# Keeping bf16 copies of the weights in DRAM: what it did to an eight-core encoder layer

## The chip, the cores and the metric

The kernel runs on all 8 cores of one Trainium2 chip. The metric is device time in microseconds (us) of the slowest core, lower is better. Each core works on two of the 16 sequences. No core talks to another, and each loads all weights for itself.

Some executions fall into a slower state: 6 of the 20 runs of the kernel before took 3124 to 3275 us, the others 2898 to 2923, and in a slow run of transfers_alone (3327 us) the four cores of one die had a mean granted clock of 0.81, the others 0.98. 12 of the 14 kernels had such runs. Ratios compare fast runs alone, of both kernels and from the same chip. The plain medians are over all runs of a kernel, slow ones too.

## The reference, cut to what matters

```python
# per layer, x: (16, 2048, 1024) float32, D_FF = 2816
x <- x + 1/2 * SwiGLU_1(RMSNorm(x))
h = RMSNorm(x); proj = h @ w_in            # one projection for all head groups
fox = forgetting attention (8 heads x 64, causal)
gla = gated linear attention (4 heads), rms-normed, times silu(g_out)
x <- x + concat(fox, gla) @ w_out
x <- x + 1/2 * SwiGLU_2(RMSNorm(x))
return RMSNorm(x)
```

The weights arrive as float32. The matmuls use bf16.

## The kernel before

A core treats its 4096 tokens as 8 groups of 512. The stages are FFN1, mixer (projections, attention, output projection) and FFN2, written f1, mixer and f2 below. The kernel does not hold the weight tiles on the chip; every group loads every weight again: 22 `wgu` tiles and 16 `wd` tiles for each FFN, 16 `mixw` tiles for the mixer. The loads go through POOL's DMA queue, which casts float32 to bf16 on the way (it wrote 344 MB, and 705 MB were read from HBM in all).

```python
wgu = sb("wgu", [128, 3, 2048], BF16)             # ring of 3
wd = sb("wd", [128, 4, NC2 * 128], BF16)          # ring of 4
mixw = sb("mixw_t", [128, 2, 2048], BF16)         # ring of 2
...
t1f = rstdM                                       # scratch of the gate tanh: the FFN norm's tile
...
wb = nxt("wgu", 3)
DMA("pool", ("wgu", wb), wgu[:, wb, :], wgu_d[f][half * NC2 + cl], 1 << 20, writes=[("wgu", wb)], ...)
...                                               # 16 matmuls of 128x512 with this tile, tanh, two products

def ffn2(tg, middle):
    ...
    norm_rstd(rstdM[:], "rstdM", b, 0)            # writes rstdM
    ...                                           # x_sb scaled by rstdM, then stored to y by SP

def mixer(tgg):
    ...
    def ev(b, h=h):                               # the output gate, 4 times a group
        tg_ = t1f
        ACTV([(tg_[:], banks[b][:], AF.Tanh, None, 0.5)], [], [PS(b), "rstdM"])
        STT(cc[:, 4 + h, :], tg_[:], 1.0, banks[b][:], ALU.add, ALU.mult, ["rstdM"], [PS(b), ("cc", 4 + h)])
```

The program does not write instructions in the order of execution. It records every operation with what it reads and writes. A planner then simulates the engines with rough durations, and each engine's fixed order comes from that plan.

## Time and profile before

| | before |
|---|---|
| median of the first 6 runs (one of them slow) | 2903.84 us (2898.38 to 3275.29) |
| TensorE (PE) busy in the profiled run | 2693.8 of 2911.3 us |
| PE idle (difference) | 217.5 us |
| of it, waiting for weight DMA (wgu, mixw, wd) | 93.9 us |

In the views, PE is TensorE's matmuls and PEld its weight loads, DVE is VectorE, ACT is ScalarE, POOL is GpSimd. SP is SyncE, which here only issues transfers. L299 is line 299 of the kernel; where a helper makes every instruction, all have its line, so go by the tiles. A `bank` is one of the eight PSUM buffers that matmuls write. "A <- B" among the waits means that A stood idle until B was done.

From the page of the kernel before: busy time by engine (us, share of the span, instructions), then the two main DMA queues (packets, MB, share of 16 engines' time), then HBM traffic.

```profile
PE 2693.8 (93%) x13328; PEld 1260.1 (43%) x13328; DVE 1464.2 (50%) x2186; ACT 1105.4 (38%) x2189; POOL 511.8 (18%) x1017
...
q0 software_dynamic: 106176, 344.07, 72.2%
q1 hardware_dynamic: 10816, 32.53, 3.5%
...
HBM read 704.84 MB, written 16.78 MB: 248 GB/s over the span
```

PE is the bottleneck, 93% busy: 64 uninterrupted matmuls of 128x512 take 14.00 us in the chain of waits, 218.8 ns each, and the granted clock is 0.98 over the span. The DMA engines come second, and 72% of their time goes to the casting queue.

From the list of waits of the kernel before, PE only: total us, times, longest.

```profile
PE bank L299 <- DMA wgu<-wgu: 60.7, 35, 12.2
PE bank L299 <- DMA mixw_t<-mixw: 31.4, 22, 4.3
PE bank L299 <- DVE x_sb L339: 21.7, 18, 2.2
...
PE bank L299 <- DMA wd<-wd: 1.8, 1, 1.8
```

From the page of the kernel before, the DMA issues: count, size, median us from issue to landing.

```profile
wgu<-wgu POOLq DMA_DIRECT2D x352, 512.0 KB, 6.3
wd<-wd POOLq DMA_DIRECT2D x256, 352.0 KB, 5.6
mixw_t<-mixw POOLq DMA_DIRECT2D x128, 512.0 KB, 6.5
```

Compare 6.3 us with the ring. A `wgu` tile feeds 16 matmuls, 3.5 us. In a ring of three, a load issued when its buffer comes free has the time of two other tiles, 7.0 us, before PE needs it. This is an estimate from the durations above, for stretches with FFN work alone.

**Four stretches.** To see where kernels differ, I cut each run by work done, not by time: the moving columns of all PE matmuls are summed, and a stretch ends when 4%, 31%, 86% and 100% of them have been streamed. The times of a stretch are medians over the 8 cores of the profiled run. The second stretch, 4% to 31%, holds nearly all of the stores that the change will add (in the trace after, about 89 of 92 on a core); the fourth is the tail, the last mixer and the last two FFN2.

The windows view of the kernel before, cut at these points on its slowest core. Columns: window, length, busy us (instructions) of PE, PEld, DVE, ACT, POOL, granted PE clock (1.00 is full), mean busy share of the 16 DMA engines, GB/s.

```profile
0.00:148.00 148.00, 113.16 (x485) 47.80 (x486) 56.56 (x79) 31.20 (x48) 27.45 (x66) 0.98 0.90 164
148.00:924.00 776.00, 723.24 (x3718) 346.17 (x3717) 421.53 (x640) 292.78 (x564) 140.98 (x280) 0.99 0.78 129
924.00:2478.00 1554.00, 1472.29 (x7299) 691.78 (x7298) 797.41 (x1192) 614.32 (x1220) 278.73 (x546) 0.98 0.77 133
2478.00:2900.00 422.00, 384.82 (x1831) 174.33 (x1828) 183.30 (x268) 164.53 (x356) 64.61 (x125) 0.96 0.65 113
```

### The profile page before, as it was taken

How to read it: one execution, taken by the hardware profiler on the slowest of the kernel's cores; microseconds unless marked ns; L12 is line 12 of the kernel's file. 1: busy time of each engine (PE TensorE's matmuls, PEld its weight loads, DVE VectorE, ACT ScalarE, POOL GpSimd, SP SyncE). 2: the span in 40 equal slices, each digit the busy share in tenths (PEclk: the TensorE clock that was granted, in tenths of full speed). 3: DMA queues.
4: the chain of work that ended last, by engine and by line, in shares of the span. 5: the costliest groups of instructions: out<-in, count | busy, mean ns of one | idle time of the engine just before them, and what ended most of it. 6: DMA issues, size and time to landing. Idle time of an engine off the chain costs nothing.

```text
span 2911.3 us, 39715 instructions; the slowest of 8 cores (2888.4 to 2911.3 us)
## 1 busy us (share of the span) xinstructions
PE 2693.8 (93%) x13328; PEld 1260.1 (43%) x13328; DVE 1464.2 (50%) x2186; ACT 1105.4 (38%) x2189; POOL 511.8 (18%) x1017
## 2 busy tenths in 40 slices
PE   5999889989999999999999889998999999999797
PEld 2445445434454444444444334543345444354233
DVE  3344845733456444554346735376253664454433
ACT  2231534521437423475234303264231662328611
POOL 1111311211112111121112211122111221111110
PEclk9999999999999999999999999999999999999999
DMA  8988767698785987767877787767887658885365
GB/s 186 143 136 140 114 106 129 109 170 141 128 140 93 177 140 129 122 123 135 137 129 130 138 160 130 133 113 147 135 134 136 111 100 137 154 139 95 75 116 111
DMA packets 117474, 380.17 MB, mean 131 GB/s; under 512 B 13327, under 2 KB 13472, under 8 KB 116384
## 3 DMA queue, kind: packets, MB, share of 16 engines
q0 software_dynamic: 106176, 344.07, 72.2%
q1 hardware_dynamic: 10816, 32.53, 3.5%
q8 instruction: 114, 1.87, 0.3%
q10 hardware_dynamic: 288, 1.05, 0.1%
q14 instruction: 80, 0.66, 0.1%
HBM read 704.84 MB, written 16.78 MB: 248 GB/s over the span
## 4 chain that ended last, share of the span: by engine, by line
PE 71%; DMA 13%; DVE 9%; issue 5%; ACT 2%; DVEq 0%; POOL 0%; SPq 0%; POOLq 0%; ACTq 0%
PE bank L299 71%; DMA wgu<-wgu 6%; DMA mixw_t<-mixw 5%; DVE hM L719 2%; DVE hF L339 2%; DVE x_sb L339 1%; DMA x_sb<-x 1%; DVE hM L339 1%; ACT hM L324 1%; DMA y<-x_sb 1%; DVE Sst L339 1%; DVE thF L339 1%; DVE Sbf L336 1%; ACT L324 1%; ACT rstdM L324 0%
## 5 line engine op out<-in xcount | busy, mean ns | idle before, releaser
L299 PE MATMUL bank<-hF,wgu 128*128 128x512 bf16 x5632 | 1306.2, 385 | 94.6 <-DMA wgu<-wgu 60.7
L299 PEld LDWEIGHTS bank<-hF,wgu 128*128 128x128 bf16 x5632 | 547.4, 99 | 775.2 <-issue 173.4
L299 PE MATMUL bank<-act,wd 128*128 128x512 bf16 x2816 | 644.0, 380 | 23.2 <-DVE x_sb L339 21.2
L324 ACT ACTIVATE thF<-bank 128x512 f32<-128x512 f32 x352 | 209.3, 597 | 830.3 <-PE bank L299 829.4
L339 DVE SCALAR_TENSOR_TENSOR thF<-thF,bank 128x512 f32<-128x512 f32 x352 | 240.7, 686 | 497.9 <-ACT thF L324 495.8
L324 ACT ACTIVATE hM<-bank,biasT 128x256 bf16<-128x256 f32 (+1 forms) x1152 | 435.7, 473 | 125.3 <-PE bank L299 124.4
L299 PEld LDWEIGHTS bank<-act,wd 128*128 128x128 bf16 x2816 | 271.5, 98 | 351.8 <-issue 37.3
L357 POOL DMA_DIRECT2D wgu<-wgu x352 | 189.8, 539 | 1134.1 <-PE bank L299 1110.8
L336 DVE TENSOR_TENSOR act<-bank,thF 128x512 bf16<-128x512 f32 x352 | 242.7, 689 | 233.6 <-PE bank L299 228.6
L339 DVE SCALAR_TENSOR_TENSOR x_sb<-bank,x_sb 128x512 f32<-128x512 f32 x256 | 173.8, 689 | 322.3 <-PE bank L299 321.2
L719 DVE RECIPROCAL hM<-bank 64x128 f32<-64x128 f32 x256 | 244.5, 955 | 65.5 <-PE bank L299 49.2
L324 ACT ACTIVATE sqF<-x_sb 128x512 bf16<-128x512 f32 x192 | 117.0, 627 | 370.9 <-DVE x_sb L339 202.4
L357 POOL DMA_DIRECT2D wd<-wd x256 | 136.8, 535 | 564.7 <-PE bank L299 563.4
L299 PE MATMUL bank<-hM,mixw_t 128*128 128x512 bf16 x896 | 205.3, 383 | 9.4 <-DMA mixw_t<-mixw 8.9
L299 PE MATMUL bank<-hM,V 128*128 128x512 bf16 (+3 forms) x640 | 199.1, 349 | 12.7 <-DVE cc L336 4.6
L299 PE MATMUL bank<-QT,KT 128*128 128x512 bf16 (+3 forms) x640 | 203.2, 350 | 1.5 <-ACT hM L324 1.5
L324 ACT ACT_TABLE_LOAD x93 | 119.3, 1283 | 125.8 <-PE bank L299 116.1
L299 PE MATMUL bank<-mixw_t,hM 128*128 128x256 bf16 x1280 | 149.0, 278 | 12.8 <-DMA mixw_t<-mixw 12.6
L357 POOL DMA_DIRECT2D mixw_t<-mixw x128 | 67.6, 528 | 478.2 <-PE bank L299 444.7
L336 POOL TENSOR_TENSOR hM<-hM,mask 128x128 bf16<-128x128 bf16 x256 | 112.0, 450 | 196.8 <-ACT hM L324 195.6
L299 PEld LDWEIGHTS bank<-mixw_t,hM 128*128 128x128 bf16 x1280 | 126.7, 100 | 37.7 <-issue 18.1
L299 PEld LDWEIGHTS bank<-hM,mixw_t 128*128 128x128 bf16 x896 | 86.8, 99 | 121.3 <-issue 22.8
(90 smaller groups left out, 1373.9 us busy)
## 6 DMA issues: line engine op xcount, KB each, us to landing
wgu<-wgu POOLq DMA_DIRECT2D x352, 512.0 KB, 6.3
wd<-wd POOLq DMA_DIRECT2D x256, 352.0 KB, 5.6
mixw_t<-mixw POOLq DMA_DIRECT2D x128, 512.0 KB, 6.5
y<-x_sb SPq DMA_DIRECT2D x64, 256.0 KB, 10.5
x_sb<-x SPq DMA_DIRECT2D x7, 2048.0 KB, 13.8
x_sb<-x ACTq DMA_DIRECT2D x2, 512.0 KB, 9.7
x_sb<-x SPq DMA_DIRECT2D x2, 512.0 KB, 9.5
wmisct<-wmisc POOLq DMA_DIRECT2D x1, 80.0 KB, 12.2
```

Source lines behind the costliest of these rows:

```text
L299: ins = e.matmul(out, lhsT=l, rhs=r, start=s0, stop=s1)
L324: ins = e.activation(out=out, in_=in_, func=func, **kw)
L336: return DVE(lambda e: e.tensor_tensor(out=out, in0=a, in1=b, op=op), free_n(out), reads, writes, rate, eng, level)
L339: return DVE(lambda e: e.scalar_tensor_tensor(out=out, in0=a, scalar=s, in1=b, op0=op0, op1=op1), free_n(out), reads, writes, level=level)
L357: return P.op(eng, lambda e: e.dma_start(out=out, in_=in_), reads, writes, dma_key=key, dur=1000.0 if eng == "pool" else 70.0, lat=100.0, ...
L719: P.op("dve", lambda e, o_=rcp[drow, qs], i_=banks[ob][srow, qs]: e.reciprocal(out=o_, in_=i_), [], [PS(ob), ("hM", 6), ("hM", 7)], dur=86 ...
```

## The change

The intent: each weight tile is cast once, stored to DRAM in bf16 at its first, second or third use, and loaded in bf16 by SP's hardware queue from then on, with half the bytes to read. 544 of 736 loads move; 92 stores are added. The change also brings four other things: a start gate (the first loads of `wd` and `mixw` and the second group's x wait for a later event than before); later x loads and y stores issued from POOL; new DMA figures in the planner; and another scratch tile for the gate tanh.

```diff
-                dma_free[e] = max(dma_free[e], t + o.dur) + o.nbytes / (o.rate * 1000.0)
-                o.end = dma_free[e] + 2000.0
+                dma_free = max(dma_free, t + o.dur) + o.nbytes / (o.rate * 1000.0)
+                o.end = dma_free + 2000.0 + o.slack
...
+    wgu_s = [dt("wgus%d" % f, [2 * NC2, 128, 2048], BF16, "Internal") for f in range(2)]
+    wd_s = [...]; mixw_s = dt("mixws", ...)
...
-        t1f = rstdM
+        t1f = sqM[:].rearrange("p r t -> p (r t)").bitcast(F32)
...
-                        dur=1000.0 if eng == "pool" else 70.0, ...
+                        dur=700.0 if eng == "pool" else 350.0, ...
...
+        def LOADW(tag, wb, tile, src, keep, i, first, reads=()):
+            key = (tag, keep.tensor.name, i)
+            use = uses.get(key, 0)
+            uses[key] = use + 1
+            kept_at = first + i % 2
+            n = 128 * free_n(tile)
+            if use > kept_at:
+                DMA("sp", (tag, wb, "b"), tile, keep[i], 2 * n, reads=[key], writes=[(tag, wb)])
+                return
+            DMA("pool", (tag, wb), tile, src[i], 4 * n, reads=reads, writes=[(tag, wb)])
+            if use == kept_at:
+                DMA("sp", (tag, wb, "s"), keep[i], tile, 2 * n, reads=[(tag, wb)], writes=[key], level=1)
...
-                    DMA("pool", ("wgu", wb), wgu[:, wb, :], wgu_d[f][half * NC2 + cl], 1 << 20, ...)
+                    LOADW("wgu", wb, wgu[:, wb, :], wgu_d[f], wgu_s[f], half * NC2 + cl, 1 - f, ...)
...  # wd and mixw likewise; their first loads gated on ("act", 5) and ("act", 10)
-            DMA("sp", ("x", xb), ..., rate=0.15)
+            DMA("sp" if tg < 3 else "pool", ("x", xb, tg < 3), ..., slack=8000.0,
+                reads=[("act", 8)] if tg == 1 else ())
...
-                DMA("sp", ("y", k % 4), ...)
+                DMA("sp" if tg < 2 or tg == NTG - 1 else "pool", ...)
...
-                        ACTV([(tg_[:], banks[b][:], AF.Tanh, None, 0.5)], [], [PS(b), "rstdM"])
+                        ACTV([(t1f, banks[b][:], AF.Tanh, None, 0.5)], [], [PS(b), ("sqM", 0), ("sqM", 1)])
```

## The prediction

> **What bounds the kernel now.** TensorE. The page gives PE 93% busy (2693.8 of 2911.3 us), with a granted clock near full speed. Uninterrupted runs in the chain (64 matmuls of 128x512 in 14.0 us) show 219 ns each; all matmuls of the by-shape list, 6.18 million streamed columns, at that rate make about 2640 us, which no DMA change can touch. What is left is 217 us in which PE is idle. The list of PE's waits splits it: weights by DMA 94 us (wgu 60.7, mixw 31.4, wd 1.8), VectorE about 74 us, ScalarE about 33 us. The chain of waits puts 11% of the span on wgu and mixw transfers, but their full flight (6.3 to 6.5 us each) mostly overlaps matmuls; the 94 us is the cost.
>
> Those 94 us by time (waits in windows): 17 us wgu in the first 60 us, about 5 to 170 us, about 8 from 170 to 560, 14.5 at 560 to 710 (the first FFN2, DMA share 0.90), and about 50 us spread over the rest.
>
> **What changes.** 544 of 736 weight loads (264 wgu, 192 wd, 88 mixw) become bf16 loads on SP; 192 remain casting loads on POOL; 92 stores (44 wgu, 32 wd, 16 mixw: 43 MB) are added, in about the first third of the span. From the queue table I work out 0.317 us per software-queue packet (3241 B written, twice that read) and 0.151 us per hardware-queue packet (3008 B): both about 20 GB/s of bytes read per engine. So the gain is the halved read, not the other queue. [...] Estimates: HBM read 705 to about 450 MB, written 17 to about 60 MB, mean DMA share 76% to about 55%; a wgu load lands in about 4 us on SP against 6.3 us. POOL loses 544 issues of 0.53 us, about 290 us of busy time, none of it critical.
>
> [...]
>
> Also: wd, mixw and second-group x loads at the start wait for later events, leaving early bandwidth to wgu; the gate's tanh scratch no longer shares the FFN norm's tile; the scheduler's DMA model changes, which reorders every engine.
>
> **On the critical path.** After about 700 us I expect DMA waits of 50 us to fall to about 8. Each removed wait also saves a pipeline refill (379 ns for an isolated matmul against 219 streaming, 0.16 us), some 6 us. The start saves about 10 us of the 22 us in the first 170 us. The first FFN2 gains nothing, perhaps loses 3 us to stores. Reordering and the scratch tile: about 10 us gain, uncertain in sign. VectorE and ScalarE waits stay near 107 us. Sum: 42 + 6 + 10 - 3 + 10, about 65 us.
>
> **Predicted:** 2838 us, range 2790 to 2882. Chances: faster by over 2% 0.6, within 2% 0.37, slower 0.03.
>
> **What would show it.** PE's waits for wgu and mixw together near 40 us, almost all before 700 us; PE idle about 150 us; PE busy almost unchanged (2670 to 2700); landing of SP weight loads under 4.5 us; HBM read near 450 MB; POOL busy near 220 us.
>
> **What would make it wrong.** [...] a load waiting for its buffer, or a store waiting for its load to land, may hold back loads behind it, as could y stores on POOL the mask products. The static order may be tightened to a modelled latency shorter than the real one, so that waits return. Freed PE time may turn into VectorE waits. [...]

## More of the kernel before

Priorities favour the mixer, so the mixer of one group runs interleaved with an FFN of another. In the record of the last groups the order is f1 of group 7, f2 of group 5, mixer of group 7, f2 of group 6, f2 of group 7.

The timeline of the kernel before, inside the tail: first PE's gate projections of the last mixer, then ACT's work on the tile `rstdM`. Columns: start us, duration us, engine, line, operation, tiles, count, idle time before it.

```profile
2430.92 3.62 PE L299 MATMUL bank<-hM,mixw_t 128*128 128x512 bf16 x16
...
2439.27 1.89 PE L299 MATMUL bank<-hM,mixw_t 128*128 128x512 bf16 x8
...
2521.78 5.34 PE L299 MATMUL bank<-hM,mixw_t 128*128 128x512 bf16 x24
```

```profile
2511.30 0.69 ACT L324 ACTIVATE rstdM<-bank,cst 128x512 f32<-128x512 f32 x1
2512.08 0.63 ACT L324 ACTIVATE rstdM<-rstdM 128x512 f32<-128x512 f32 x1
...
2520.09 0.60 ACT L324 ACTIVATE rstdM<-bank 128x512 f32<-128x512 f32 x1 [2.95 <-DVE x_sb L339]
2521.73 0.60 ACT L324 ACTIVATE rstdM<-bank 128x512 f32<-128x512 f32 x1 [1.04 <-DVE cc L339]
```

Here the mixer projects three gate tiles (24 matmuls) by 2441 us and then its projections stand still for 80 us. The first two ACT lines (`rstdM<-bank,cst` and `rstdM<-rstdM`) are the norm of the FFN2 that runs beside it; the tanhs (`rstdM<-bank`) follow only after that norm's scaling of `x_sb`.

## The result, and the profile after

| | before | after |
|---|---|---|
| median, slow runs included | 2910.95 us (20 runs) | 2871.69 us (10 runs) |
| ratio of fast runs, 95% interval | | 0.9872 (0.9851 to 0.9892) |
| PE busy, profiled run | 2693.8 of 2911.3 us | 2679.0 of 2867.6 us |
| PE waits for weight DMA | 93.9 us | 71.9 us |
| HBM read / written | 704.84 / 16.78 MB | 451.09 / 59.77 MB |

A ratio is the mean time of one kernel's fast runs over the mean of the other's fast runs of the same rounds, so it is not quite the ratio of the medians. The kernel is 1.3% faster, about 37 us; 65 us were predicted.

The same lines of the page after:

```profile
PE 2679.0 (93%) x13328; PEld 1261.7 (44%) x13328; DVE 1467.6 (51%) x2186; ACT 1104.2 (39%) x2189; POOL 251.1 (9%) x518
...
q1 hardware_dynamic: 95920, 308.34, 32.9%
q0 software_dynamic: 31760, 111.26, 21.9%
...
HBM read 451.09 MB, written 59.77 MB: 178 GB/s over the span
```

PE's waits after; `wgus`, `wds` and `mixws` are the kept copies.

```profile
PE bank L303 <- DMA mixw_t<-mixw: 33.6, 12, 8.4
...
PE bank L303 <- DMA wgu<-wgu: 21.3, 9, 11.9
...
PE bank L303 <- DMA wgu<-wgus: 6.0, 3, 2.8
```

The DMA issues after:

```profile
wgu<-wgus SPq DMA_DIRECT2D x264, 512.0 KB, 3.5
...
wgu<-wgu POOLq DMA_DIRECT2D x88, 512.0 KB, 7.4
...
wgus<-wgu SPq DMA_DIRECT2D x44, 512.0 KB, 5.9
mixw_t<-mixw POOLq DMA_DIRECT2D x40, 512.0 KB, 8.2
```

The kept loads land in 3.5 us, a little under the estimated 4, and PE seldom waits for them. The loads that still cast have become slower: 6.3 to 7.4 us for `wgu`, 6.5 to 8.2 us for `mixw`. Those after are all early ones, those before come from the whole run. Counted in the second stretch alone (all cores), the medians rise as well: 6.1 to 7.7 and 6.5 to 7.8 us.

Which of them PE waits for is another question. PE's weight waits in the second stretch, before (148 to 924 us), then after (148 to 981 us):

```profile
PE bank L299 <- DMA wgu<-wgu: 15.8, 9, 5.8
...
PE bank L299 <- DMA mixw_t<-mixw: 6.4, 6, 2.4
```

```profile
PE bank L303 <- DMA mixw_t<-mixw: 33.6, 12, 8.4
PE bank L303 <- DMA wgu<-wgu: 6.8, 5, 2.3
```

The waits that grow are above all those for the mixer's tiles, whose ring has two buffers. Those for `wgu` shrink, although the casting `wgu` load now exceeds the 7.0 us of its ring. On medians of the 8 cores, all weight waits of this stretch together rise from 19 to 48 us.

The windows after, cut at the same work:

```profile
0.00:148.00 148.00, 112.51 (x487) 48.13 (x488) 56.56 (x79) 31.10 (x48) 26.78 (x66) 0.95 0.90 167
148.00:981.00 833.00, 742.91 (x3721) 350.45 (x3720) 423.22 (x641) 300.61 (x579) 124.52 (x235) 0.96 0.78 170
981.00:2480.00 1499.00, 1456.38 (x7377) 696.90 (x7376) 799.70 (x1197) 606.90 (x1208) 76.10 (x169) 0.99 0.43 138
2480.00:2855.00 375.00, 366.84 (x1748) 166.16 (x1746) 182.77 (x263) 163.01 (x352) 23.70 (x48) 1.00 0.40 127
```

The small net gain is a large loss and two large gains. On medians of the 8 cores:

| stretch (share of columns) | before | after | difference |
|---|---|---|---|
| to 4% | 147.0 | 151.2 | +4.2 |
| 4% to 31% | 773.6 | 825.6 | +52.0 |
| 31% to 86% | 1548.1 | 1498.6 | -49.4 |
| 86% to end | 418.5 | 375.2 | -43.3 |

In the second stretch PE is busy for 743 us instead of 723 us with the same number of streamed columns, and idle 90 us instead of 53. The mean DMA share is 0.78 in both, over a longer time. The busy part goes with the clock, 0.96 against 0.99: in this stretch it stands at 0.50 for 58 us instead of 22 (medians of the cores). On the slowest cores PE is busy at 0.50 for 51 us instead of 15; half of that difference is 18 of the 20 us (an estimate from the clock and matmul records). In 8 of the 9 PE waits of over 3 us on the slowest core after, the clock drops to 0.50 within 5 us of the wait's start, so a long wait is paid for again, in part. The windows after, during the longest DMA wait, show how (it lies in the first stretch; PE starts at 68.7 us again, after 11.9 us idle):

```profile
60.00:64.00 4.00, 0.00 (x0) 0.00 (x0) 0.00 (x0) 0.00 (x0) 0.00 (x0) 0.50 1.09 225
64.00:72.00 8.00, 3.28 (x8) 1.16 (x9) 0.00 (x0) 0.00 (x0) 0.00 (x0) 0.50 0.99 269
```

The clock is 0.50 from 60 to 72 us, through the first 3 us of the work that follows, and 0.79 from 72 to 76 us. In the second stretch, around the longest wait there (8.4 us), it is 0.56 from 646 to 656 us. These are means over the windows: the clock records of before and after hold 0.50 and 1.00 alone.

The tail, in the timelines after (PE, then ACT):

```profile
2421.14 3.62 PE L303 MATMUL bank<-hM,mixw_t 128*128 128x512 bf16 x16
2428.21 5.34 PE L303 MATMUL bank<-hM,mixw_t 128*128 128x512 bf16 x24
```

```profile
2425.11 0.60 ACT L328 ACTIVATE sqM<-bank 128x512 f32<-128x512 f32 x1 [4.74 <-DVE ft L340]
2427.08 0.59 ACT L328 ACTIVATE sqM<-bank 128x512 f32<-128x512 f32 x1
```

The last mixer's tanhs now follow its projections within 4 us, and the mixer goes on.

### The profile page after: what moved, and what is told of

Its sections match the earlier page's. It is cut to its first block, busy times and chain, and to the rows that moved or that the text cites. A ratio compares the mean times of both kernels' runs of the same rounds, so it can differ in the third digit from the quotient of the medians.

```text
span 2867.6 us, 40029 instructions; the slowest of 8 cores (2853.4 to 2867.6 us)
## 1 busy us (share of the span) xinstructions
PE 2679.0 (93%) x13328; PEld 1261.7 (44%) x13328; DVE 1467.6 (51%) x2186; ACT 1104.2 (39%) x2189; POOL 251.1 (9%) x518
## 3 DMA queue, kind: packets, MB, share of 16 engines
HBM read 451.09 MB, written 59.77 MB: 178 GB/s over the span
## 4 chain that ended last, share of the span: by engine, by line
PE 75%; DMA 11%; DVE 8%; issue 4%; ACT 2%; POOL 0%; DVEq 0%; SPq 0%; ACTq 0%; POOLq 0%
PE bank L303 75%; DMA mixw_t<-mixw 4%; DMA wgu<-wgu 3%; DVE hM L740 2%; DVE hF L343 2%; DVE x_sb L343 1%; DVE Sst L343 1%; DMA wgus<-wgu 1%; DMA wd<-wd 1%; DVE hM L343 1%; DMA wgu<-wgus 1%; DVE Sbf L340 1%; ACT L328 1%; DVE thF L343 1%; ACT rstdM L328 0%
## 5 line engine op out<-in xcount | busy, mean ns | idle before, releaser
L303 PE MATMUL bank<-hF,wgu 128*128 128x512 bf16 x5632 | 1290.5, 382 | 63.3 <-DVE thF L343 21.3
L303 PE MATMUL bank<-act,wd 128*128 128x512 bf16 x2816 | 651.6, 383 | 32.3 <-DVE x_sb L343 22.6
L340 POOL TENSOR_TENSOR hM<-hM,mask 128x128 bf16<-128x128 bf16 x256 | 118.6, 476 | 1511.2 <-ACT hM L328 1510.8
L303 PE MATMUL bank<-cc,mixw_t 128*128 128x512 bf16 x512 | 123.0, 390 | 12.2 <-DMA mixw_t<-mixw 10.8
L303 PEld LDWEIGHTS bank<-hM,V 128*128 128x128 bf16 x640 | 62.3, 98 | 89.0 <-issue 28.4
L303 PEld LDWEIGHTS bank<-QT,KT 128*128 128x128 bf16 x640 | 61.7, 98 | 66.0 <-issue 8.1
```

Source lines behind the costliest of these rows:

```text
L303: ins = e.matmul(out, lhsT=l, rhs=r, start=s0, stop=s1)
L340: return DVE(lambda e: e.tensor_tensor(out=out, in0=a, in1=b, op=op), free_n(out), reads, writes, rate, eng, level)
```

## The experiments

**Theory A:** the stores, and the casting loads that run beside them, cost the 52 us; the halved loads give the 49 us; the new order gives the 43 us at the tail. **Rival R:** the new order costs the 52 us, and the transfers give the rest. Further rivals came up on the way: the queue of x and y, the buffer that a store holds, the planner's figures, the scratch tile.

All stretch medians in one table; each run is described below.

| run | to 4% | to 31% | to 86% | tail | ratio to before (95%) |
|---|---|---|---|---|---|
| before | 147.0 | 773.6 | 1548.1 | 418.5 | 1 |
| after | 151.2 | 825.6 | 1498.6 | 375.2 | 0.9872 (0.9851 to 0.9892) |
| transfers_alone | 147.0 | 834.5 | 1495.6 | 407.8 | 0.9968 (0.9923 to 1.0012) |
| rest_alone | 150.8 | 792.6 | 1606.6 | 396.4 | 1.0196 (1.0155 to 1.0238) |
| store_twice | 150.9 | 909.0 | 1502.1 | 375.2 | 1.0142 (1.0073 to 1.0211) |
| copy_beside | (152.7) | (1012.8) | (1512.6) | (375.3) | 1.0541 (1.0509 to 1.0572) |
| xy_on_sp | 151.3 | 825.2 | 1509.4 | 375.4 | 0.9886 (0.9837 to 0.9935) |
| spread4 | 150.2 | 819.2 | 1515.8 | 375.7 | 0.9900 (0.9883 to 0.9918) |
| no_keep | 151.4 | 783.5 | 1546.2 | 387.5 | 0.9939 (0.9922 to 0.9955) |
| mix_cast | 150.5 | 820.6 | 1504.0 | 373.9 | none: too few fast runs |
| half_keep | 150.2 | 816.2 | 1524.4 | 381.0 | 0.9936 (0.9913 to 0.9959) |
| half_ffn_old_gates | 146.1 | 795.4 | 1518.9 | 386.2 | 0.9856 (0.9833 to 0.9880) |
| plan_only | 146.6 | 778.1 | 1548.0 | 419.5 | 1.0006 (0.9989 to 1.0023) |
| scratch_only | 147.5 | 780.1 | 1535.3 | 385.9 | 0.9852 (0.9833 to 0.9871) |

All twelve variants gave correct results. Numbers in brackets are from a profile in the slow state; its cores are looked at below.

### 1. transfers_alone: the new transfers in the old order

```diff
 # the kernel before, with LOADW and the three DRAM tensors, and in the planner:
+    P.op("sp", <load keep[i]>, ..., dur=1000.0, nbytes=4 * n, meng="pool")   # planned as the old load
+    P.op("sp", <store keep[i]>, ..., ghost=True)                             # planned at no cost
```

> The kernel before with the new transfers alone: stores and bf16 loads on SP as in the change, while the planner still sees the old loads, so TensorE, VectorE and ScalarE run their instructions in exactly the order of before; x, y, start gates and tanh scratch as before. Stretches are cut by the share of streamed columns that TensorE has done (4%, 31%, 86%, all); before takes 147 / 773 / 1548 / 419 us, after 151 / 825 / 1499 / 375. Theory A (the stores and the mix of casting loads and stores cost the 52 us between 4% and 31%, the halved loads give the 50 us between 31% and 86%, the new order gives the 43 us at the end): here about 147 / 820 / 1500 / 413, in all about 2880 + 17, ratio to before near 1.00. Rival R (the new order costs the 52 us, the transfers give the rest): 147 / 773 / 1500 / 380, ratio near 0.97.

Measured: 147.0 / 834.5 / 1495.6 / 407.8, ratio 0.9968. The first three stretches are as theory A has them. Rival R falls: with the order of before, unchanged instruction by instruction on PE, VectorE and ScalarE, the loss is +60.9 us. The gain in the third stretch is -52.5 us. At the tail, the transfers account for 10.6 of the 43 us. The headline idea of the change, by itself, is worth nothing that the interval can tell from zero.

The DMA issues of this run show the same slowing of the loads that still cast:

```profile
wgu<-wgus SPq DMA_DIRECT2D x264, 512.0 KB, 3.6
...
wgu<-wgu POOLq DMA_DIRECT2D x88, 512.0 KB, 7.2
```

### 2. rest_alone: the new order with the old transfers

```diff
 # the change, but
-    DMA("sp", (tag, wb, "b"), tile, keep[i], ...)
+    P.op("pool", <casting load src[i]>, ..., dur=350.0, nbytes=2 * n, meng="sp")  # planned as the new load
-    DMA("sp", (tag, wb, "s"), keep[i], tile, ...)
+    P.op("sp", None, ..., phantom=True)     # in the plan, dropped from the program
```

> The changed kernel with its order, gates, scratch tile and x and y queues, but every weight load is the old casting load on POOL and no store is made: TensorE, VectorE and ScalarE run in exactly the order of after. Theory A: stretches about 150 / 778 / 1548 / 378 us, ratio to before near 0.985; casting loads meet a plan that expects shorter ones, so the third stretch may also be worse than before. Rival R: 150 / 825 / 1548 / 414, ratio near 1.015.

Measured: 150.8 / 792.6 / 1606.6 / 396.4, ratio 1.0196. The total is near R's, but not for R's reason: the second stretch loses 19 us, a third of what the transfers alone lose, and the tail gains 22 us. The surprise, which neither theory had, is the third stretch, +58.5 us: a static order planned for short loads does badly with long ones (PE waits 89 us for `wgu` and `mixw` there on the slowest core, 41 us before). What it costs that these loads stand in POOL's queue at places planned for SP's is not separated. So order and transfers do not add up as two separate effects: -2 and +59 by themselves, -36.5 together.

### 3. store_twice: the suspected cost doubled

```diff
 # the change, and at every store
+    P.op("sp", <store spare[i] from the same tile>, reads=[(tag, wb)], ..., ghost=True)
```

> The changed kernel with each of the 92 stores made twice, the second to a DRAM tensor that nothing reads (43 MB more written), without cost in the plan, so every other engine keeps its order. Theory A: the stretch from 4% to 31% grows from 825 to about 860 to 880 us, the others stay within 5 us; ratio to before about 1.00. Rival R: under 8 us more anywhere, ratio near 0.988.

Measured: 150.9 / 909.0 / 1502.1 / 375.2, ratio 1.0142. The second stretch alone grows, by 83.4 us, more than expected. The first set of stores went with a loss of 61 us (transfers_alone; this is net of the bf16 loads that already run in this stretch), the next set costs 83. The windows view of the second stretch and the issues of this run:

```profile
154.00:1062.00 908.00, 761.87 (x3721) 353.84 (x3720) 422.56 (x640) 300.30 (x577) 124.17 (x235) 0.93 0.87 202
```

```profile
wgu<-wgu POOLq DMA_DIRECT2D x88, 512.0 KB, 8.7
```

The DMA share rises from 0.78 to 0.87, a casting `wgu` load to 8.7 us, and the clock falls to 0.93.

### 4. xy_on_sp: x and y back on SP

```diff
-    eng = "sp" if tg < 3 else "pool"            # x; y likewise
+    real engine "sp", planned as in the change
```

> The changed kernel with all x loads and y stores issued by SP as before, planner unchanged, so all other engines keep their order. In the trace of after an x load on POOL waits 10 us for y stores and two mixw loads stand behind it in POOL's queue, which ends in an 8.4 us TensorE wait. If that queue is a main part of the loss, the stretch from 4% to 31% falls by 12 us or more (825 to 813 or less) and the late stretches grow by little; if it is not, all stretches stay within 6 us, or the late ones grow because SP's weight loads now stand behind x and y.

Measured: 151.3 / 825.2 / 1509.4 / 375.4. The second stretch does not move. So the wait seen behind an x load on POOL is not a main part of the loss, and the queue of x and y does not make the tail either. The third stretch is 10.8 us longer.

### 5. copy_beside: the bytes without the buffer

By the recorded dependencies a store also holds its weight buffer until it has landed, so the next load into it waits (61 us of POOL's time in the second stretch after, see below). Here the second transfer is a copy from DRAM to DRAM of the same size, which holds nothing.

```diff
-    P.op("sp", <store spare[i] from tile>, reads=[(tag, wb)], ...)
+    copy = P.op("sp", <copy spare[i] from src[i]>, [], ...); copy.after = load   # waits for the load only
```

> As the run with every store made twice, at the same places of SP's queue and behind the same waits, but the second transfer copies the same number of bytes from the weights in DRAM to the spare DRAM tensor and so holds no weight buffer: the next load into the buffer waits for one store, not two. After takes 151 / 825 / 1499 / 375 us in the four stretches, the doubled store 151 / 909 / 1502 / 375. If the stores cost through the bytes that the 16 shared DMA engines move, the second stretch is 890 us or more here (a copy also reads DRAM, so up to 925). If they cost through the weight buffer that they hold, it is below 845. Between: both, in proportion.

Measured: the second stretch takes 1012.8 us. The profile fell in the slow state (a core of the slow die shows a clock of 0.81 through its tail, 2781 to 3230 us), so look at the four cores of the undisturbed die: 998 to 1017 us, against 817 to 834 us for the same four cores after, about 178 us more by their medians. So transfers that hold no buffer cost time. That the buffer plays no part is not shown: the stores beside the copies land later too (`wgus`: 10.0 to 10.5 us on this die, 5.7 to 6.0 after), so they hold their buffers longer. In the second stretch POOL stands still, ready to load again into a buffer but for a store that has not landed, for 61 us after, 122 us in store_twice and 167 us here (medians of the cores; here of the undisturbed die). The copy costs even more than the second store (about 178 against 83 us). It also reads 43 MB from DRAM, and the queue tables give it more engine time: summing both queues' shares times the span, store_twice adds 159 us of all 16 engines to after, copy_beside 250 us (this one from a slow-state profile). How much of a store's cost is holding the buffer stays open, and so does whether the transfers crowd each other on the 16 DMA engines or in the DRAM: no run separates these.

### 6. spread4: the same stores over four groups

```diff
-            kept_at = first + i % 2
+            kept_at = first + i % 4
```

> The changed kernel with the stores spread over four uses (first + i % 4) instead of two: the same 92 stores, but half as many per token group, and 448 bf16 loads instead of 544; the planner plans anew. If what hurts is the crowding of stores and casting loads in a few groups, the loss shrinks: second stretch about 800 us, third about 1515, whole kernel about 2860, ratio 0.982. If each store costs the same wherever it stands, the 52 us only move: second stretch about 805, third about 1530, whole kernel 2880 or more, ratio 0.990 or above.

Measured: 150.2 / 819.2 / 1515.8 / 375.7, ratio 0.9900. The second stretch falls by only 6.4 us and the third grows by 17.2. Spreading does not win the loss back; delaying the stores mostly moves and adds cost. As 88 loads more still cast here (the trace has 456 bf16 loads, not the 448 of the expectation), crowding alone is not isolated.

### 7. no_keep: everything but the keeping, planned for it

```diff
-            kept_at = first + i % 2
+            kept_at = 99
```

> The changed kernel with the keeping of weights switched off (no stores, every load casts on POOL), and the planner told so: what the other parts of the change (one DMA timeline in the planner, gates at the start, scratch tile, x and y on POOL) do by themselves. If the 43 us at the end come from the planner's new DMA model alone, the last stretch is about 376 us and the kernel gains: 150 / 780 / 1550 / 378, ratio near 0.985. If they come from planning with short loads, the last stretch stays near 410 and the kernel is within 10 us of before.

Measured: 151.4 / 783.5 / 1546.2 / 387.5, ratio 0.9939. Without any kept weight, 31 of the 43 us at the tail are there. Against this run, keeping the weights adds 42 us in the second stretch, takes 48 in the third and 12 at the tail: a net gain of 18 us.

### 8. mix_cast: the mixer's weights not kept

```diff
-    LOADW("mixw", wb, mixw[:, wb, :], mixw_d, mixw_s, i, 1, ...)
+    LOADW("mixw", wb, mixw[:, wb, :], mixw_d, mixw_s, i, 99, ...)
```

> The changed kernel with the mixer's weights never kept (16 stores and 88 bf16 loads less, planned anew). The mixer's ring has two buffers, and most of TensorE's waits in the second stretch of after are for casting mixer loads (some 34 us). If the stores on that short ring are the main cost there, the second stretch falls from 825 to about 800 us, at the price of some 10 to 20 us more mixer waits in the third (1499 to about 1515). If all stores cost alike, the second stretch falls by about 16/92 of 52, some 9 us, and the kernel is slower than after.

Measured: 150.5 / 820.6 / 1504.0 / 373.9 in a fast profile. Only 2 of its 6 timed runs were fast (2869.3 and 2869.6 us), so there is no ratio. By the stretches, keeping the mixer's weights is worth about nothing: leaving them out saves 5 us where the stores fall and loses 5 us later. It also cuts POOL's waits for stores in the second stretch from 61 to 19 us, for these 5 us. This suggests, without showing it, that held buffers are not the main cost.

### 9. half_keep: every other tile

```diff
-            kept_at = first + i % 2
+            kept_at = first + i // 2 % 2 if i % 2 == 0 else 99
```

> The changed kernel, but only every other weight tile is kept (even i, stored at use first or first + 1), the rest cast at each use; planned anew. 48 stores, about half of the kept loads. If the stores cost through the bytes on the DMA engines while those are nearly full, and the late gain saturates because the engines are then far from full (DMA share 0.42 in after), half of the stores should cost about half of the 42 us that keeping adds to the second stretch (no_keep 783, after 825: here about 803) and give more than half of the 48 us of the third (no_keep 1546, after 1499: here about 1512). Stretches about 151 / 803 / 1512 / 377, ratio near 0.984. If gain and cost both go in proportion, 151 / 804 / 1523 / 381, ratio about 0.990.

Measured: 150.2 / 816.2 / 1524.4 / 381.0, ratio 0.9936. Half the stores (46 by the kernel's indices, not the 48 of the expectation) still cost 33 of the 42 us (against no_keep) and give less than half of the 48 us. The guess that cost halves while most of the gain stays was wrong in both parts.

### 10. half_ffn_old_gates: the attempt at a better kernel

```diff
 # half_keep, and
-    LOADW("mixw", ..., i, 1, ...)
+    LOADW("mixw", ..., i, 99, ...)
-    first wd, mixw and second x loads wait for ("act", 5), ("act", 10), ("act", 8)
+    they wait as in the kernel before
```

> As half_keep, but the mixer's weights are never kept (the run before showed that keeping them gains nothing), and the start gates are those of the kernel before (first wd, mixw and second-group x loads not held back). If the new gates are what costs the 4 us at the start, the first stretch returns to 147 us. Otherwise about 800 / 1515 / 378 in the rest: ratio near 0.982, the best of all runs if it holds. If the start stays at 151, the gates are not the cause.

Measured: 146.1 / 795.4 / 1518.9 / 386.2, ratio 0.9856 (0.9833 to 0.9880). Die 1 of this profile was disturbed for part of the time (61 to 215 us a core at a clock of 0.81); the four cores of die 0 alone give 145.7 / 794.7 / 1521.5 / 386.2. The start is back. In all runs, those with the new gates take 150 to 153 us to 4%, and those with the old gates 146 to 148 us. The ratio of 0.982 that was hoped for is missed, above all at the tail. The kernel beats before, but its interval overlaps that of the change.

### 11. plan_only: the planner's figures alone

```diff
 # the kernel before, with
+    one dma_free for all queues; 700 / 350 ns an issue; slack 8000 for x
```

> The kernel before with nothing but the planner's new DMA figures (one DMA timeline for all queues, 700 ns and 350 ns an issue, 8 us of slack for x instead of a low rate): no kept weights, old gates, old scratch tile, x and y on SP. If the planner's figures alone make the 31 us that the run without kept weights gained at the end, the last stretch is about 388 us here too and the kernel is about 25 us faster than before (ratio 0.991). If it is the scratch tile or the queues of x and y, the last stretch stays above 410.

Measured: 146.6 / 778.1 / 1548.0 / 419.5, ratio 1.0006. The planner's figures do nothing by themselves. The tail keeps its 419 us. With xy_on_sp (not the queues) and half_ffn_old_gates (not the gates), the scratch tile is left, and the traces point at it: all runs with a short tail have the new tile.

### 12. scratch_only: one tile renamed

```diff
 # the kernel before, with
-        t1f = rstdM
+        t1f = sqM[:].rearrange("p r t -> p (r t)").bitcast(F32)
 # and its users reading and writing ("sqM", 0), ("sqM", 1) instead of "rstdM"
```

> The kernel before with only the tile of the mixer's gate tanh changed (the squares' tile instead of the FFN norm's reciprocal-root tile). In before the last mixer's gate projection starts at 2431 us, but its tanh runs at 2520 us, after the norm of the FFN beside it (2511 us) has used the shared tile; in all runs with the new tile it follows the projection within some us (2421 to 2425 in after), in all with the old tile it comes after the norm. If this sharing is what makes the tail: last stretch about 388 us instead of 419, tanh before 2460 us, the other stretches within 5 us of before, ratio near 0.989. If it is not: last stretch above 410, ratio within 0.003 of 1.

Measured: 147.5 / 780.1 / 1535.3 / 385.9, ratio 0.9852 (0.9833 to 0.9871). The tail is as expected, and the third stretch gains another 12.8 us, which was not expected. The window of the tail in this run, and its ACT timeline there:

```profile
2472.00:2857.00 385.00, 370.36 (x1814) 171.69 (x1812) 183.68 (x268) 163.22 (x351) 62.77 (x124) 1.00 0.73 124
```

```profile
2428.47 0.60 ACT L324 ACTIVATE sqM<-bank 128x512 f32<-128x512 f32 x1 [3.60 <-DVE ft L336]
2430.00 0.60 ACT L324 ACTIVATE sqM<-bank 128x512 f32<-128x512 f32 x1 [0.94 <-PE bank L299]
```

PE idles 15 us in the tail instead of 37, while every weight is still cast at every use and the DMA share is 0.73. PE's waits there for anything but DMA fall from 24 to 7 us on the slowest cores, those for DMA stay at 8. This one rename is measured as large as the whole change; the intervals overlap, so I do not claim that it is larger.

Read beside no_keep it says more. no_keep has the same new tile, and besides it the planner's figures, the start gates and the x and y queues of the change. It is slower than scratch_only: the intervals, 0.9922 to 0.9955 and 0.9833 to 0.9871, lie apart, and the stretches differ by 20 us (4 at the start, 11 in the third). So on this path the scratch tile gives 38 us, the other small parts cost 20 us, and the keeping gives 18 us. Which of the small parts costs is separated at the start only, and the scratch tile with the keeping alone was never run.

Why it works: the gate tanh of the last mixer is recorded after the f2 of group 5, and both wrote `rstdM`. The tanh therefore had to wait for the end of that FFN2's norm. With three PSUM banks (output buffers of TensorE) for the mixer and three gate tiles projected into them, the mixer stopped from 2441 to 2521 us, and what it could not run beside that FFN2 was left for the tail, where too little other PE work remained. With its own scratch, the mixer runs beside it.

## Why the prediction was right or wrong

- **PE bounds the kernel, and weight waits are 94 us: right.** HBM traffic (451 read, 60 written), landing of kept loads (3.5 us), mean DMA share (about 55%) and PE busy (2679 us) came out as predicted. POOL's busy time was 251 instead of about 220 us. PE's idle time was 189 us (2867.6 minus 2679.0), not near 150, and its waits for `wgu` and `mixw` 62 us, not near 40. That the gain is the halved read and not the other queue rests on the packets' times (0.317 us for 3241 B written and twice that read, 0.151 us for 3008 B without a cast, worked out from the queue table of before); a cost of the cast itself is not separated from this.
- **"After about 700 us I expect DMA waits of 50 us to fall to about 8", with 6 us of refills: right in size, but later.** The third stretch, which starts at 924 us before, gains 52.5 us with the transfers alone, and PE's weight waits in it fall from 41 to 5 us in the change. But between 700 and 981 us after there are 20 us of them, more than the 8 that were to be left; before has none from 700 to 924 us. The 6 us of refills were my estimate, from the 379 ns that one matmul's record takes (the median of the `wgu` matmuls) and the 219 ns between streamed ones; no run measures them by themselves.
- **"The first FFN2 gains nothing, perhaps loses 3 us to stores": the step that failed most.** The term measured 61 us with the transfers alone, 42 us against no_keep. I did place the stores in the first third of the span, but gave them a cost in the first FFN2 only, and judged the traffic by its mean over the span (DMA share 76% to 55%). What matters is where they fall: in a stretch whose casting loads already keep the DMA engines at a share of 0.78 and land with little to spare (6.3 of 7.0 us for `wgu`). There the casting loads land later (`wgu` 7.4, `mixw` 8.2 us), PE waits for the mixer's above all, and long waits are paid for again, in part, in half clock (58 us at 0.50 in this stretch instead of 22).
- **"The start saves about 10 us": wrong in sign.** It costs 4 us. In the first 170 us `wgu` waits fall from 20.4 to 14.5 us, but 7.4 us of waiting for `hF` appear and those for `wd` grow from 1.8 to 4.6 us. That the gates are to blame rests on how the 14 kernels fall on two sides, with no run of the gates alone. The nearest pair is half_keep and half_ffn_old_gates (150.2 and 146.1 us); their other difference, the mixer's keeping, does not move the start by itself (mix_cast, 150.5 us).
- **"Reordering and the scratch tile: about 10 us gain, uncertain in sign": wrong in size.** The scratch tile alone gives about 38 us by the stretches. The planner's figures alone give none. I costed the tile as a short conflict between two instructions. It was an order between an entire FFN2 and a mixer.
- **The warnings.** A static order tightened to short loads does bring waits back when loads are long (rest_alone, +58.5 us), but in the change loads are short where it counts. SP did wait for casting `wgu` loads (332.6 us in 37 waits after, the longest 80.6), but of PE's waits only 10.7 us are for kept loads. The queue of x and y did not matter much (xy_on_sp: 825.2 against 825.6 us in the second stretch, 10.8 us more in the third).

The sum in the end: about +4 at the start, +52, -49 and -43, where I had -10, +3 or so, -48 and -10. Two mis-sized terms of opposite sign make the total look nearer than its parts were: that it lies inside the range of 2790 to 2882 us is luck. The parts interact, so no exact split of the 37 us between keeping and scratch can be given: keeping is worth -2 us in the old order and -18 us on top of the rest.

The trace after shows the two main queues sharing the time of the 16 DMA engines: in slices of 2 us on its slowest core either queue alone reaches a share of 1.07 to 1.08, and both together never more than 1.08, with a median of 1.02 in the 95 slices in which each takes over a quarter. This agrees with the loss: with stores on SP's queue, loads on POOL's landed in 7.4 us instead of 6.3 and, with the stores doubled, in 8.7 us.

## What to carry to other kernels

Here a transfer's price was set by the stretch in which it ran (the 92 stores went with 42 to 61 us in a stretch at a DMA share of 0.78): ask there whether the loads that the bottleneck waits for still fit into their ring's time, and look which of them it does wait for. When a change bundles several edits, run each alone; here a renamed scratch tile carried as much as the idea in the title. In a program whose order comes from recorded dependencies, a scratch tile shared by two stages is an ordering between the stages: look for work that stands still while its inputs have long been ready.
